# A mixture of softmaxes on one core: the first unit is loaded in one transfer of four heads instead of four transfers of one head

## The chip, the core and the metric

The kernel runs on one core of one Trainium2 chip. Its engines work side by side, each through its own list of instructions: TensorE for matmuls (PE in the profile, with PEld for its weight loads), VectorE (DVE), ScalarE (ACT), GpSimd (POOL) and SyncE (SP), which does no arithmetic and issues transfers. The transfers themselves are run by 16 DMA engines between HBM and the core's memory. The metric is the device time of one execution in microseconds (us); lower is better.

## What is computed

```python
batch, seq, vocab, num_heads = 32, 128, 4096, 4
# logits: (batch, seq, heads, vocab) f32, prior: (batch, seq, heads) f32
prior_probs = np.exp(prior - prior.max(axis=-1, keepdims=True))
prior_probs = prior_probs / prior_probs.sum(axis=-1, keepdims=True)
softmax = np.exp(logits - logits.max(axis=-1, keepdims=True))
softmax = softmax / softmax.sum(axis=-1, keepdims=True)
mixture = np.sum(prior_probs[..., None] * softmax, axis=2)   # over the 4 heads
```

For each of 32 x 128 rows, four rows of 4096 logits (the heads) become four softmaxes, which are added with the weights of a softmax over `prior`. The input is 32 x 8 MiB and the output 32 x 2 MiB. There is little arithmetic for each byte.

## The kernel before, in words

A *unit* u is one of the 32 batch entries: 128 rows on the 128 partitions, with four heads of 4096 f32 (16 KB a row and head, 2 MiB a head). `ring` is a buffer of 12 slots of one head each, so it holds three units. Head h of unit u lies in slot 4u + h modulo 12, except the very last head. `acc` is the whole PSUM, 128 x 4096 f32: one unit's sum. Columns are cut in four quarters of 1024, and a matmul covers 512 of them.

The order of all work is written by hand as a text of words. A word is a letter, digits, and a unit: `'` is the unit before, `+2` the unit two later, `@26` unit 26, and nothing is the unit of the text itself. The letters and their lines:

- **L** (`load`, line 120): loads heads a to b on SP's queue. Heads whose slots lie side by side go in one transfer; `L` alone is all four heads, `L03` heads 0 to 2, `L34` head 3 alone. **S** (`store`, line 125) stores the unit; for units 2 to 21 on ACT's queue, otherwise on SP's.
- **M** (`peak`, line 128, DVE): the negated maximum of one head. **E** (`exp`, line 133, ACT): the exponential of one head in place, with its sum. **R** (`recip`, line 139, DVE): the reciprocal of the sum.
- **G** (`diagonal`, line 142, POOL): a 128 x 128 diagonal matrix of the row weights prior / sum. **X** (`weigh`, line 151, PE): adds one head, times that matrix, into `acc`; heads 0 to 2 go this way.
- Head 3: **C** (line 158, POOL) makes its row weight and **Z** (line 162, POOL) scales its later columns.
- Joining: for the first quarter or two, **A** (line 168, DVE) adds head 3 and `acc`. For the other quarters **V** (line 187, ACT) copies `acc` out and **P** (line 190, POOL) adds the scaled head 3. Both write into the slot of head 3, and from there the unit is stored.

Each text handles heads of unit u and joins unit u - 1 in between. For unit 1 the text is:

```python
"M0 E0 R3' C3' Z314' M1 R0 G0 A01' V12' P12' V23' P23' V34' P34' E1 X0 S' L03+2 L34+2 "
"M2 E2 R1 G1 X1 M3 E3 R2 G2 X2 "
```

An engine takes the instructions of its own letters in this order. So on SP the store of unit u - 1 comes after its last P, then the loads of unit u + 2, which go into the slots that unit u - 1 leaves: `L03+2` behind the joins, `L34+2` behind the end of the store. From unit 24 on the order is a longer list of words with unit numbers.

Ahead of the texts, line 208 runs the words in `FIRST` for unit 0. Line 209 issues the load of `prior` on ACT's queue. Line 210 loads unit 1 with `L`. Lines 218 to 228 compute the prior's softmax, five steps on DVE and one on ACT, and transpose it to `pp` on DVE. All this stands ahead of `M0` of unit 0 in DVE's list. The text for unit 0 then has `L03+2 L34+2`, the loads of unit 2, which need no free slot and so wait for nothing.

Of the kernel before, what the change touches and what calls it, by code (L numbers as in the profile page):

```python
# [22 lines left out]

FIRST = "L01 L12 L23 L34"
STEADY = (
    "M0 E0 R3' C3' Z324' M1 R0 G0 A01' A12' V23' P23' V34' P34' E1 X0 S' L03+2 L34+2 "
    "M2 E2 R1 G1 X1 M3 E3 R2 G2 X2 "
# [43 lines left out]
def kernel(  # L73
# [124 lines left out]
    def run(u, words):  # L198
        for w in words.split():
            op, digits, back, on, at = re.fullmatch(  # L200
                r"([A-Z])(\d*)('*)(?:\+(\d+))?(?:@(\d+))?", w
            ).groups()
            v = int(at) if at else u - len(back) + int(on or 0)
            if 0 <= v < U:
                step[op](v, *map(int, digits))

    with tc.manual_schedule():
        run(0, FIRST)
        nc.scalar.dma_start(out=pr, in_=prior)
# [53 lines left out]
```

## Time and profile before

| | |
|---|---|
| median of 3 runs | 787.47 us (787.11 to 787.48) |
| the profiled execution | 786.99 us |
| its span, from the first instruction to the last | 785.2 us |
| busiest engines, share of the span | PE 86%, DVE 82%, ACT 70%, POOL 38% |
| moved by DMA | 335.90 MB, 428 GB/s over the span |
| granted TensorE clock, mean | 0.965 |

Times in the views count from the span's start. A row of the timeline has the start, the duration, the engine, the line, the operation, what it writes and reads, how often it is merged into that row, and in brackets how long the engine sat idle before it and what ended that. A row of DMA issues has what is moved, the queue, how often, the size of each, and the median time from issue to landing. In the list of queues, a row has the number of packets, the MB, and the share of 16 engines' time that the packets took.

### The profile page before, as it was taken

To read this page: it belongs to the slowest core of one execution; us is meant where nothing else is said; L and a number is where in the kernel's file an instruction comes from. 1 tells how busy PE (TensorE), PEld (TensorE's weight loads), DVE (VectorE), ACT (ScalarE), POOL (GpSimd) and SP (SyncE) were. 2 spreads that over 40 slices of the span, in tenths; PEclk is the share of its full clock that TensorE was granted. 3 is DMA by queue.
4 is the path that set the end of the run, shared out by engine and by line. 5 is a ranking of instruction groups with operands and counts; after the bars stand their busy time and mean duration, and the time that the engine had idled before them with its cause. 6 is when DMAs were issued, how large, how long until landed. Compare 5 with 4: busy or idle time off the path is not lost.

```text
span 785.2 us, 4590 instructions
## 1 busy us (share of the span) xinstructions
PE 679.0 (86%) x1508; PEld 291.8 (37%) x1508; DVE 644.2 (82%) x326; ACT 548.0 (70%) x327; POOL 296.9 (38%) x244
## 2 busy tenths in 40 slices
PE   0959998888998989989889898998978998899996
PEld 0424444333443333434334333343333433334342
DVE  6489877897778977779877798777888877979895
ACT  2566876867668666687676776766857668779883
POOL 0053333433134332334323343323430544277892
PEclk9979999999999999989999999999989999999999
DMA  9999999999999999999999999999999999999998
GB/s 377 451 417 426 452 416 423 431 446 430 437 417 432 440 437 437 427 420 437 444 422 446 410 435 451 425 431 420 432 440 442 425 418 431 444 419 429 429 427 340
DMA packets 15336, 335.90 MB, mean 428 GB/s; under 512 B 1713, under 2 KB 1713, under 8 KB 2257
## 3 DMA queue, kind: packets, MB, share of 16 engines
q1 hardware_dynamic: 12384, 293.61, 87.1%
q10 hardware_dynamic: 2928, 42.01, 12.5%
q8 instruction: 12, 0.20, 0.1%
q14 instruction: 12, 0.09, 0.0%
HBM read 268.50 MB, written 67.11 MB: 427 GB/s over the span
## 4 chain that ended last, share of the span: by engine, by line
DMA 58%; DVE 12%; PE 10%; POOL 10%; issue 6%; ACT 3%; SPq 0%; POOLq 0%; ACTq 0%
DMA ring<-in_logits_dram 58%; DVE nmax L128 12%; PE acc L151 10%; POOL ring L190 7%; ACT ring L187 2%; ACT ring L133 1%; POOL ring L184 1%; POOL ring L162 1%; POOL diag L142 1%; DVE ring L168 0%; SPq L120 0%; DVE rden L139 0%; SPq L125 0%; POOLq L190 0%; POOLq L142 0%
## 5 line engine op out<-in xcount | busy, mean ns | idle before, releaser
L151 PE MATMUL acc<-ring,diag 128*128 128x512 f32 x1508 | 679.0, 611 | 99.3 <-ACT ring L187 63.7
L128 DVE TENSOR_REDUCE nmax<-ring 128x1 f32<-128x4096 f32 x128 | 563.1, 4409 | 115.9 <-DMA ring<-in_logits_dram 115.9
L133 ACT ACTIVATE ring<-ring,nmax 128x4096 f32<-128x4096 f32 x128 | 474.6, 3708 | 203.7 <-DVE nmax L128 203.3
L151 PEld LDWEIGHTS acc<-ring,diag 128*128 128x128 f32 x1508 | 291.8, 196 | 485.6 <-issue 356.3
L190 POOL TENSOR_TENSOR ring<-ring 128x1024 f32<-128x1024 f32 x69 | 162.3, 2371 | 19.6 <-ACT ring L187 12.9
L142 POOL TENSOR_SCALAR diag<-ident,rden,pp 128x128 f32<-128x128 f32 x96 | 42.9, 448 | 237.5 <-DVE rden L139 237.5
L158 POOL TENSOR_TENSOR wght<-rden,pp 128x1 f32<-128x1 f32 x33 | 6.2, 189 | 209.5 <-DVE rden L139 209.5
L187 ACT ACTIVATE ring<-acc 128x1024 f32<-128x1024 f32 x69 | 67.4, 1010 | 16.2 <-PE acc L151 12.0
L162 POOL TENSOR_SCALAR ring<-ring,rden,pp 128x2048 f32<-128x2048 f32 (+3 forms) x35 | 75.1, 2146 | 9.4 <-DVE rden L139 9.4
L168 DVE SCALAR_TENSOR_TENSOR ring<-ring,wght,acc 128x1024 f32<-128x1024 f32 x59 | 73.2, 1270 | 3.0 <-PE acc L151 1.3
L139 DVE RECIPROCAL rden<-dsum 128x1 f32<-128x1 f32 x128 | 19.3, 153 | 10.1 <-ACT ring L133 10.1
L133 ACT ACTIVATION_READ_ACCUMULATOR ring<-ring,nmax 128x1 f32 x128 | 24.2, 189 | 0.0
L184 POOL TENSOR_TENSOR ring<-ring 128x1024 f32<-128x1024 f32 x5 | 11.9, 2373 | 0.1
L218 DVE TENSOR_REDUCE pmax<-pr 32x128 f32<-32x512 f32 x1 | 0.7, 674 | 5.2 <-DMA pr<-in_prior_dram 5.2
L220 ACT ACTIVATE pr<-pr 32x512 f32<-32x512 f32 x1 | 0.6, 628 | 4.1 <-DVE pr L219 4.1
L168 DVE SCALAR_TENSOR_TENSOR ring<-ring,wght 128x1024 f32<-128x1024 f32 x2 | 2.5, 1283 | 0.3 <-POOL wght L158 0.3
L220 ACT ACT_TABLE_LOAD x1 | 1.3, 1283 | 1.2 <-PEq L247 1.2
L227 DVE STREAM_TRANSPOSE pp<-pn 32x128 f32<-32x128 f32 x4 | 1.2, 302 | 0.1
L221 DVE TENSOR_REDUCE pmax<-pr 32x128 f32<-32x512 f32 x1 | 0.7, 674 | 0.7 <-ACT pr L220 0.7
L223 DVE TENSOR_TENSOR pn<-pr,pmax 32x512 f32<-32x512 f32 x1 | 1.0, 1021 | 0.0
L222 DVE RECIPROCAL pmax<-pmax 32x128 f32<-32x128 f32 x1 | 0.9, 942 | 0.0
L219 DVE TENSOR_TENSOR pr<-pr,pmax 32x512 f32<-32x512 f32 x1 | 0.7, 680 | 0.0
(6 smaller groups left out, 0.9 us busy)
## 6 DMA issues: line engine op xcount, KB each, us to landing
ring<-in_logits_dram SPq DMA_DIRECT2D x27, 6144.0 KB, 34.3
ring<-in_logits_dram SPq DMA_DIRECT2D x43, 2048.0 KB, 25.9
out_dram<-ring ACTq DMA_DIRECT2D x20, 2048.0 KB, 16.0
out_dram<-ring SPq DMA_DIRECT2D x11, 2048.0 KB, 14.0
out_dram<-ring SPq DMA_DIRECT2D x4, 512.0 KB, 5.5
pr<-in_prior_dram ACTq DMA_DIRECT2D x1, 64.0 KB, 4.4
ring<-in_logits_dram SPq DMA_DIRECT2D x1, 39.4
```

The lines of the kernel that those rows point to most:

```text
L128: nc.vector.tensor_reduce(out=nmax[:, u, h : h + 1], in_=slot(u, h), op=ALU.max, axis=AX.X, negate=True)
L133: nc.scalar.activation(slot(u, h), slot(u, h), AF.Exp, bias=nmax[:, u, h : h + 1], accum_out=dsum[:, u, h : h + 1],)
L139: nc.vector.reciprocal(rden[:, u, h : h + 1], dsum[:, u, h : h + 1])
L142: nc.gpsimd.tensor_scalar(out=diag[:, u % 2, h], in0=ident, scalar1=rden[:, u, h : h + 1], scalar2=pp[:, h, u : u + 1], op0=ALU.mult, op1= ...
L151: nc.tensor.matmul(acc[:, k * W : (k + 1) * W], lhsT=diag[:, u % 2, h], rhs=e[:, k * W : (k + 1) * W], start=h == 0, stop=h == H - 2 or (u ...
L158: nc.gpsimd.tensor_mul(wght[:, u, h : h + 1], rden[:, u, h : h + 1], pp[:, h, u : u + 1])
L162: nc.gpsimd.tensor_scalar(out=e, in0=e, scalar1=rden[:, u, h : h + 1], scalar2=pp[:, h, u : u + 1], op0=ALU.mult, op1=ALU.mult,)
L168: nc.vector.scalar_tensor_tensor(out=o, in0=slot(u, h, a, b), scalar=wght[:, u, h : h + 1], in1=more, op0=ALU.mult, op1=ALU.add,)
L184: nc.gpsimd.tensor_add(e, e, slot(u, 2, a, b))
L187: nc.scalar.activation(slot(u, 1, a, b), acc[:, a * C : b * C], AF.Copy)
L190: nc.gpsimd.tensor_add(home(u, a, b), slot(u, 1, a, b), slot(u, 3, a, b))
L220: nc.scalar.activation(pr, pr, AF.Exp)
```

## The change

`FIRST` held four words, one for each head of unit 0. It now holds one word for all four heads:

```diff
-FIRST = "L01 L12 L23 L34"
+FIRST = "L"
```

`load` (line 115) joins heads whose slots lie side by side, and unit 0's four heads are in slots 0 to 3:

```python
while h + n < to and place(u, h + n) == s + n:
    n += 1
nc.sync.dma_start(out=ring[:, s : s + n], in_=logits[u, :, h : h + n, :])
```

SP's list therefore begins with one transfer of 128 rows of 64 KB, the form that unit 1 has in both kernels, where it had four transfers of 128 rows of 16 KB. All heads of unit 0 now wait for the end of this one transfer. SP issues 3 instructions fewer. Instructions of the other engines, and their order, are the same in both kernels; only which transfer's semaphore they wait for differs.

## The prediction, as recorded before the result was known

> **What bounds the kernel now.** I read the page first, for what is full; then the chain of waits, for what is late each round; then the first 72 us of the timeline, the only place that the diff touches; then the DMA issues and packets there.
>
> ```profile
> DMA  9999999999999999999999999999999999999998
> PEclk9979999999999999989999999999989999999999
> HBM read 268.50 MB, written 67.11 MB: 427 GB/s over the span
> ```
>
> The DMA engines are at 90% or more in every slice but the last. The same list of queues asked for 20 to 760 us alone says more:
>
> ```profile
> DMA packets 13713, 319.22 MB, mean 431 GB/s; under 512 B 1520, under 2 KB 1520, under 8 KB 1520
> q1 hardware_dynamic: 10810, 276.99, 87.0%
> q10 hardware_dynamic: 2880, 41.94, 13.3%
> ```
>
> 87.0 + 13.3 is all of the 16 engines' time: there is no gap to speak of between 20 and 760 us. The chain of waits repeats one round of 48.5 us for two units, 34.3 us of it a load waiting in this queue. So the time is what the queue needs for its bytes, plus its start and its end. A change in the first microseconds counts only if it alters the time that rows take in the queue, or if it makes the queue run dry later. An engine that is late costs nothing as long as a transfer is queued.
>
> The start, from the timeline of 0 to 75 us:
>
> ```profile
> 5.23 0.67 DVE L218 TENSOR_REDUCE pmax<-pr 32x128 f32<-32x512 f32 x1 [5.23 <-DMA pr<-in_prior_dram]
> ...
> 11.33 8.75 DVE L128 TENSOR_REDUCE nmax<-ring 128x1 f32<-128x4096 f32 x2
> ...
> 20.84 22.34 PE L151 MATMUL acc<-ring,diag 128*128 128x512 f32 x48 [20.84 <-POOL diag L142]
> ...
> 24.45 4.40 DVE L128 TENSOR_REDUCE nmax<-ring 128x1 f32<-128x4096 f32 x1
> ...
> 42.33 4.42 DVE L128 TENSOR_REDUCE nmax<-ring 128x1 f32<-128x4096 f32 x1 [13.41 <-DMA ring<-in_logits_dram]
> ...
> 50.49 2.83 ACT L187 ACTIVATE ring<-acc 128x1024 f32<-128x1024 f32 x3
> ...
> 51.72 7.00 POOL L190 TENSOR_TENSOR ring<-ring 128x1024 f32<-128x1024 f32 x3
> ...
> 58.75 0.35 SPq L125 DMA_DIRECT2D out_dram<-ring  x1
> ...
> 59.26 8.11 SPq L120 DMA_DIRECT2D ring<-in_logits_dram  x2
> ```
>
> The reader is to see the slack. The prior's steps keep DVE to 11.33. Then the four maxima of unit 0 (the last at 24.45) run without a wait for data, and after 28.85 DVE is idle for 13.41 us until unit 1 lands. Joining unit 0 (lines 187 and 190) starts only behind unit 1's first maxima and exponential, at 50.49. Unit 0's store is issued at 58.75 and the first load of unit 3 at 59.26: the first moment at which the queue depends on any compute.
>
> **What the transfers cost.** Three rows of DMA issues, each from a short window around its issue (at 2.15, 3.65 and 4.05 us), and the queue in 10 to 20 us and in 24 to 40 us:
>
> ```profile
> ring<-in_logits_dram SPq DMA_DIRECT2D x1, 2048.0 KB, 20.8
> ```
>
> ```profile
> ring<-in_logits_dram SPq DMA_DIRECT2D x1, 6144.0 KB, 53.4
> ring<-in_logits_dram SPq DMA_DIRECT2D x1, 2048.0 KB, 57.8
> ```
>
> ```profile
> q1 hardware_dynamic: 299, 4.37, 102.7%
> ```
>
> ```profile
> q1 hardware_dynamic: 112, 7.34, 106.0%
> ```
>
> Head 3 of unit 0, issued at 2.15, lands at 22.95; unit 2 lands at 57.0 and 61.9. Of the 299 packets, 32 are the 4-byte ends of transfers, so a 16 KB row takes 1.027 x 160 / 267 = 0.615 us of one engine. A 64 KB row takes 1.060 x 256 / 112 = 2.42 us. A transfer has 128 rows, eight for each engine.
>
> **The change, part by part.**
>
> 1. *Bytes.* Unit 0 takes 4 x 8 x 0.615 = 19.69 us of each engine now and 8 x 2.42 = 19.38 us as one transfer: -0.3 us for the queue, and all behind it lands 0.3 us earlier. The single end marks are about 0.01 us each, nothing. Bounds: 0 (startup, where rows take longer than later, may eat it) and -0.4. I take -0.3, as unit 1 shows that very form. Unit 0 then lands at 22.65 and unit 1 at 42.0.
>
> 2. *SP's issues.* Three fewer, of 0.33 to 0.7 us each in SP's list; all seven are through by 4.40, and the queue has work until 61. Hidden; the cover is the queue itself. The first transfer starts its rows about 1.0 us after its issue at 0.79 (first packets at 1.8 in the trace), and that stays.
>
> 3. *The prior's load* is the one thing that shares the start. Its 32 rows of 2 KB, two on each engine, and an end mark each took a turn between 16 KB rows, and it lands 4.4 us after its issue. Turns between 64 KB rows cost up to three times 2.42 - 0.615 = 1.8 us more, 5.4 in all: it lands at 10.6, and DVE's 6.1 us (5.23 to 11.33) end at 16.7. A fourth turn makes it 19. Both are before 22.65. Hidden, with 4 to 6 us to spare.
>
> 4. *Unit 0's work* starts at 22.65 instead of 11.33: 11.3 us late. The maxima end at 40.2 instead of 28.85, still before unit 1 lands at 42.0, so DVE takes unit 1 on time. ACT ends unit 0's last exponential at about 43.9, before unit 1's first at 46.5. PE is what comes late: its 48 matmuls run from 32.1 to 54.5 instead of 20.84 to 43.18. The second quarter of columns is done eight matmul records (0.43 us each at full clock, from the spacing of the weight loads) before the end, at 51.1, where ACT could have copied it at 50.2. So the three copies start at 51.1, 52.8 and 54.5, not back to back, and ACT's next exponential moves by 2.3 us. POOL's first add starts at 52.05 instead of 51.4 (both with the 0.3 us of part 1); the other two follow without a wait, since each takes 2.34. Unit 0's store is issued at about 59.1 instead of 58.75.
>
> 5. *Is the queue still full then?* The last rows of unit 2 leave the first engine at 60.93 (the 16 end marks lie between 60.93 and 61.28 in the packets), now 60.6. A store issued at 59.1 has rows ready 1.0 us later, by the one row for that, the first transfer of the run: 60.1. Half a microsecond is left of what was 1.2. No gap, +0. Bounds: 0 and +0.5, if the issue takes half as long again and the estimate of 59.1 is 0.5 us early.
>
> 6. *What is late next.* Queued behind the late copies on ACT are unit 1's exponentials, and DVE waits for them: 2.3 us. PE gains it back. In the row of stretches below it sat idle from 43.2 to 52.6, and its granted clock is 0.50 from 48 to 57, about ten matmuls at 0.86 us. With unit 1 directly behind unit 0 at 54.5 there is no such pause; 48 x 0.43 = 20.6 brings it to 75.1, where it ends at 75.26 now. Unit 1's store, at 80.40 now, hangs on that, and the queue then has work until head 3 of unit 3 lands at 88.7. DVE's 2.3 us go into its idle time at 70 to 80 (2.7 us). Nothing reaches the queue: +0.
>
> ```profile
> 48.00:50.00 2.00, 0.00 (x0) 0.00 (x0) 2.00 (x1) 2.00 (x1) 1.97 (x1) 0.50 0.91 393
> ```
>
> The end of the program is the same work at the same distance from the last bytes, so it moves with the queue. Sum: 785.2 - 0.3 = 784.9 of span, with the 1.8 us around it 786.7; the profiled execution was 0.5 below the median of the three runs, so **787.2** as a median.
>
> **The rivals.**
>
> *The prior is starved, and the kernel is slower.* If the prior's rows do not get their turn until an engine is through its eight rows of unit 0, the prior lands at about 22.5 and DVE starts unit 0 at 28.6, 17.3 us late instead of 11.3. The copies and adds move by 6.0, the store to 65.1, its rows to 66.1: the queue is dry for 5.5 us, and the time is 792.7. It decides as soon as the prior lands after 16.5. Against it: between 16 KB rows, with 32 of them queued on each engine ahead, the prior landed after 4.4 us. [...] The Trainium skill (DMA: Bandwidth & Descriptors, section Queues, rings and completion order) says that an engine drains a whole packet, typically 9 to 17 descriptors, from one queue before it goes to the next. With eight rows on each engine that would be this rival; the packets of this trace are single rows, and turns came after each. Chance 0.08.
>
> *The queue runs dry at unit 0's store* for a smaller reason: unit 0 lands later than 22.65 or its chain is slower. Half a microsecond is covered, and every further one costs one. To be seen as slower (over 0.2%, 1.6 us, about what a measurement of this kernel can tell from no change) it takes a store at 61.2. Time 789.2, chance 0.08. Most smaller cases are within 0.2%.
>
> *Fewer transfers are worth more, and the kernel is faster.* The first transfer landed 7.5 us after issue, of which 4.9 are rows; if each hand-over between transfers cost those 2.6 us, three fewer give 779.7. The heads of unit 0 land at 8.3, 13.1, 18.2 and 22.95 (issue plus time to landing), hardly more apart than the 4.9 us of their rows, so a hand-over costs about nothing. Chance 0.05.
>
> **How the numbers follow.** My forecast, hidden with -0.3 us, has 0.79; its own range, from the bounds of parts 1 and 5, and the spread of the three runs, is 786.4 to 788.1. To hold 8 in 10 the range reaches into the dry queue: 786.2 to 789.2. Faster by over 0.2% has 0.06 (the hand-over, and what I have not seen), slower 0.15 (the two slow rivals, less the small end of one), the same 0.79.
>
> **What the profile of the changed kernel would show.** The first maximum (line 128) starts at about 22.6 with a DMA wait before it; the second wait for unit 1, now 13.41 us, shrinks to about 2. The prior's first step starts between 10 and 13: after 16.5 the first rival holds. PE's clock has no dip between 47 and 57. Unit 0's store is issued at about 59.1 and unit 3's first load lands near 82.4 (82.7 now); if it lands past 83.5, the queue ran dry. I am wrong if unit 0 lands after 24.5, if the prior comes late, or if the later rounds are not fixed by the queue alone.

## The result, and the profile after

The change makes the kernel a little slower: 788.29 us median (787.36 to 789.38, 20 runs) against 787.11 us (786.50 to 787.89, 20 runs), a ratio of 1.0016 with a 95% interval of 1.0010 to 1.0022. That is 1.2 us. It lies within the 0.2% that I had set as no change and within the range, but clear of noise, and on the other side of the 0.3 us gain that I had forecast.

The profiled execution after took 787.88 us, its span 786.2 us, 1.0 us more than before. DMA engines and clock look as before on the page; the difference has to be looked for in the first 70 us. The landings first, from the page and from a short window around the first issue:

```profile
pr<-in_prior_dram ACTq DMA_DIRECT2D x1, 64.0 KB, 10.5
```

```profile
ring<-in_logits_dram SPq DMA_DIRECT2D x1, 22.6
```

Unit 0, issued at 0.79, lands at 23.4 (22.95 for its last head before, 22.65 forecast). The prior lands at 11.3 and is not in the way. Then the timeline of the start:

```profile
23.39 8.74 DVE L128 TENSOR_REDUCE nmax<-ring 128x1 f32<-128x4096 f32 x2 [6.03 <-DMA ring<-in_logits_dram]
...
32.91 49.32 PE L151 MATMUL acc<-ring,diag 128*128 128x512 f32 x110 [32.91 <-POOL diag L142]
...
42.75 4.42 DVE L128 TENSOR_REDUCE nmax<-ring 128x1 f32<-128x4096 f32 x1 [1.77 <-DMA ring<-in_logits_dram]
...
52.28 1.02 ACT L187 ACTIVATE ring<-acc 128x1024 f32<-128x1024 f32 x1 [1.28 <-PE acc L151]
...
53.45 7.01 POOL L190 TENSOR_TENSOR ring<-ring 128x1024 f32<-128x1024 f32 x3 [1.28 <-ACT ring L187]
...
60.50 0.35 SPq L125 DMA_DIRECT2D out_dram<-ring  x1
```

It goes as forecast as far as unit 1, which DVE takes on time after a wait of 1.77 us. PE no longer pauses between the units. But the first copy of unit 0 waits for PE until 52.28, the adds run from 53.45, and the store is issued at 60.50: 1.75 us later than before, where I had said 0.35. What this does to the queue is in the stretches 61.0 to 62.5 and 65 to 67 us, before and then after; the last two columns are the DMA engines' share and the GB/s:

```profile
61.00:62.50 1.50, 1.50 (x5) 0.70 (x4) 1.50 (x3) 0.94 (x1) 0.45 (x1) 1.00 1.15 492
65.00:67.00 2.00, 2.00 (x6) 0.81 (x5) 2.00 (x3) 1.42 (x3) 0.94 (x2) 1.00 1.26 524
```

```profile
61.00:62.50 1.50, 1.50 (x5) 0.74 (x4) 1.50 (x1) 1.50 (x1) 0.12 (x1) 1.00 0.88 371
65.00:67.00 2.00, 2.00 (x6) 0.85 (x5) 2.00 (x1) 2.00 (x1) 0.45 (x1) 1.00 1.27 385
```

At 61, where the queue passes from the loads of unit 2 to the store of unit 0, it moves 371 GB/s instead of 492, and at 65 to 67, the end of that store, 385 instead of 524. The single packets in the trace say what it is: the engines that are through first sit idle for up to 0.3 us at 61, and the last two rows of the store take 0.8 and 1.1 us on average (1.2 at most) instead of 0.61. From the last 4-byte end mark of unit 2 to that of the store it takes 5.82 us instead of 4.95. The queue was not to be without work before unit 0's store, and this is where it was.

### The profile page after: what moved, and what is told of

It reads as the page before. It is cut to its first block, busy times and chain, and to the rows that moved or that the text cites. A ratio compares the mean times of both kernels' runs of the same rounds, so it can differ in the third digit from the quotient of the medians.

```text
span 786.2 us, 4582 instructions
## 1 busy us (share of the span) xinstructions
PE 677.5 (86%) x1508; PEld 291.3 (37%) x1508; DVE 643.9 (82%) x326; ACT 548.3 (70%) x327; POOL 296.9 (38%) x244
## 4 chain that ended last, share of the span: by engine, by line
DMA 60%; DVE 13%; POOL 10%; PE 7%; ACT 5%; issue 5%; SPq 0%; POOLq 0%
DMA ring<-in_logits_dram 60%; DVE nmax L128 12%; POOL ring L190 7%; PE acc L151 7%; ACT ring L133 3%; ACT ring L187 2%; POOL ring L184 1%; POOL ring L162 1%; POOL diag L142 1%; DVE ring L168 0%; DVE rden L139 0%; SPq L125 0%; POOLq L190 0%; POOLq L142 0%
## 5 line engine op out<-in xcount | busy, mean ns | idle before, releaser
L218 DVE TENSOR_REDUCE pmax<-pr 32x128 f32<-32x512 f32 x1 | 0.7, 674 | 11.3 <-DMA pr<-in_prior_dram 11.3
```

## Experiments

**Which part of the change is it?** Two theories stood against each other. *Late start*: with all heads of unit 0 behind one landing, its store comes when the queue is about to run dry. *Row form*: rows of 64 KB at the start, or the prior between them, cost time themselves (unit 0's last end mark was at 22.93 in this trace, 22.49 before). I ran both kernels again, and two that part these.

The kernel before, unchanged:

> The kernel before, unchanged, beside itself: ratio 1.000, within 0.0005 either way. Its trace tells which stretched rows of the DMA queue come back from run to run: unit 0's store and head 3 of unit 3 (64 to 67 us and 84 to 88 us) were stretched by 0.1 and 0.25 us in the first trace of before, and by 0.8 and 1.1 us in the trace of the change. If they were chance, they move in this trace; if they hang on when the store is issued, they stay small here.

Measured: 1.0000 (0.9991 to 1.0009). Store issued at 58.77, unit 0's last end mark at 22.51, the same two places hardly stretched. It is the same kernel twice, and in this second trace the stretches are where they were and as small.

The change, unchanged:

> The change, unchanged, for a second trace: ratio 1.001 to 1.002 again. Late-start theory (the store of unit 0 comes to the queue just as it runs out): store issued at about 60.5, unit 0's store and head 3 of unit 3 stretched again by 0.8 and 1 us. Chance theory: the stretches are elsewhere or gone, and only the 0.4 us of unit 0's landing is left.

Measured: 1.0019 (1.0010 to 1.0028). Here the store is issued at 61.24, and the hole is plain:

```profile
61.24 0.35 SPq L125 DMA_DIRECT2D out_dram<-ring  x1
```

```profile
61.00:62.50 1.50, 1.50 (x5) 0.69 (x4) 1.34 (x2) 1.50 (x3) 0.66 (x2) 1.00 0.42 175
65.00:67.00 2.00, 2.00 (x6) 0.82 (x5) 2.00 (x3) 1.33 (x1) 0.45 (x1) 1.00 1.28 393
```

175 GB/s: the last end mark of unit 2 is at 61.24 and the store's first row starts at 62.09, 0.85 us after its issue. And unit 0's last end mark is at 22.46 in this trace: the later landing of the first trace does not come back, while the slowness does.

Four loads of one head, with head 0 last:

```diff
-FIRST = "L01 L12 L23 L34"
+FIRST = "L34 L23 L12 L01"
```

> Four loads of one head for unit 0 as before, but head 0 last: work on unit 0 starts at 22.95 as in the change, while the rows stay 16 KB and the prior lands at 5.2. Late-start theory: the store is issued at 60.1 to 60.5 and the kernel is slower by 0.5 to 0.8 us (ratio 1.0006 to 1.0010), the change's loss less the 0.4 us of the landing. Row theory (64 KB rows at the start cost the time): ratio 1.000, within 0.0004.

Measured: 1.0017 (1.0008 to 1.0026), the whole of the change's loss and more than I had left for it, with 16 KB rows and the prior on time. Work starts at 23.00, the store is issued at 60.87, the queue moves 350 GB/s in 61.0 to 62.5 and 262 in 65 to 67. The row theory falls.

Two loads of two heads:

```diff
-FIRST = "L01 L12 L23 L34"
+FIRST = "L02 L24"
```

> Unit 0 in two loads of two heads (32 KB rows): work starts at about 13.2, the third maximum at about 22.7 instead of 20.06, so unit 0's store stays at 58.7 to 59.0. Late-start theory: no more than the landing's share, ratio 1.000 to 1.0003. Row theory: about half of the change's loss, ratio 1.0006 to 1.0009, with unit 0 landing 0.2 us later than in the kernel before.

Measured: 0.9999 (0.9990 to 1.0008). Work starts at 13.25, the third maximum waits 0.88 us for its load, and the store is issued at 58.73. Half the transfers, and over the eleven executions nothing lost. The one that was profiled was the slowest of them, 787.85 us. In its trace the last two rows of the store of unit 0 took 0.7 and 0.8 us on average, and head 3 of unit 3 ended about 1 us later than in the kernel before. So rows can stretch without a late store; a late store makes it the rule.

**Does a late start cost as such, or only through the store?** Five more runs. Head 0 third, so that work starts at 18.2:

```diff
-FIRST = "L01 L12 L23 L34"
+FIRST = "L23 L12 L01 L34"
```

> Head 0 of unit 0 is loaded third: its work starts at 18.2, 6.9 us later than before and 4.8 us earlier than in the change. Dry-queue theory: PE is through unit 0 at 50 to 51.5 us, no copy waits for it, the store stays at 58.7 to 58.8, and the ratio is 1.000 within 0.0005: nothing of 6.9 us is paid. Rival, every late microsecond costs its share: 6.9 of 11.6 of the change's loss, ratio 1.0010.

Measured: 0.9999 (0.9990 to 1.0008), store at 58.96. PE's end moves by 6.9 us and nobody waits for it: of a loss in proportion there is no sign.

The kernel before with its start on time, but two copies and adds of unit 0 behind an exponential of unit 1 (in the text for unit 1):

```diff
-... A01' V12' P12' V23' P23' V34' P34' E1 X0 S' L03+2 L34+2 "
+... A01' V12' P12' E1 V23' P23' V34' P34' X0 S' L03+2 L34+2 "
```

> The kernel before, with unit 0 loaded by heads and started at 11.3, but two of unit 0's copies and adds moved behind unit 1's second exponential, so that its store is issued at 60.7 to 61.3. Dry-queue theory: the queue has a gap of 0.5 to 1 us after 61, the store's last rows are stretched, and the ratio is 1.0010 to 1.0018, as if the start had been late. Rival (the late start itself costs): 1.000 within 0.0005.

Measured: 1.0031 (1.0019 to 1.0043, six executions), more than expected; the direction is as the dry queue has it. Why it costs more than the change, with a store as late, no run here tells. The store is issued at 61.02:

```profile
61.02 0.35 SPq L125 DMA_DIRECT2D out_dram<-ring  x1
```

```profile
61.00:62.50 1.50, 1.50 (x5) 0.55 (x4) 1.50 (x3) 1.24 (x1) 0.85 (x2) 1.00 0.52 218
65.00:67.00 2.00, 2.00 (x6) 0.95 (x5) 2.00 (x3) 1.41 (x2) 1.24 (x2) 1.00 1.15 336
```

The same hole and the same stretched end, without any change to the loads of unit 0.

The change with its late start, but unit 0 joined on DVE in all four quarters:

```diff
-    "M0 E0 R3' C3' Z314' M1 R0 G0 A01' V12' P12' V23' P23' V34' P34' E1 X0 S' L03+2 L34+2 "
+    "M0 E0 R3' C3' M1 R0 G0 A01' A12' A23' A34' E1 X0 S' L03+2 L34+2 "
```

> The change, with unit 0 joined in all four quarters on DVE and none through ACT and POOL: the start stays late (23), but the store can go at 57.0 to 58.0, before the queue runs out at 61. Dry-queue theory: no gap, ratio 1.000 within 0.0005. Rival (late start costs in another place too): 1.0012 to 1.0019, as the change.

Measured: 1.0000 (0.9991 to 1.0009). Work starts at 22.88, as late as in the change, and the loss is gone. The join no longer goes through POOL, whose three adds took 7.0 us in a row:

```profile
51.03 3.64 DVE L168 SCALAR_TENSOR_TENSOR ring<-ring,wght,acc 128x1024 f32<-128x1024 f32 x3
...
54.93 1.28 DVE L168 SCALAR_TENSOR_TENSOR ring<-ring,wght,acc 128x1024 f32<-128x1024 f32 x1 [0.26 <-PE acc L151]
...
56.30 0.35 SPq L125 DMA_DIRECT2D out_dram<-ring  x1
```

The store goes at 56.30, earlier than expected and 5.0 us ahead of unit 2's first end mark, at 61.33. A second run of it:

> The change with unit 0 joined on DVE, again: store issued at 56 to 58, no gap, ratio 1.000 within 0.0005. If the late start costs beside the store, it is 1.001 or more in one of the two.

Measured: 0.9995 (0.9986 to 1.0004), store at 56.65.

The kernel before with that join:

> The kernel before with the same join on DVE: store at about 56.3 instead of 58.75. Dry-queue theory: the queue was full anyway, ratio 1.000 within 0.0005, and the comparison with the run above is then level. Rival (an earlier store is a gain of its own): up to 2.4 us faster, ratio 0.997.

Measured: 1.0004 (0.9995 to 1.0013), store at 56.15. An earlier store is no gain where the queue was full.

**Where does it begin to cost?** Only the last copy and add behind the exponential:

```diff
-... V34' P34' E1 X0 S' L03+2 L34+2 "
+... E1 V34' P34' X0 S' L03+2 L34+2 "
```

> As the late-store run, with only the last copy and add of unit 0 behind unit 1's second exponential: store issued at 59.4 to 59.8, 0.7 to 1.0 us later than before, and its rows ready 0.85 us after that, at 60.3 to 60.6, just before the first engine is through unit 2 (60.9). Dry-queue theory: no gap, the store's last rows not longer than before, ratio 1.000 within 0.0005. Rival (every late microsecond of this store costs): about 40% of the late-store run, ratio 1.0012.

Measured: 1.0014 (1.0005 to 1.0023), where I had expected nothing. Store at 59.57, and no hole: 470 GB/s in 61.0 to 62.5. Again:

> The milder late store again, for a second trace and time, since the first was slower (1.0014) with no gap in the queue. Gap theory: the 1.0014 was chance, now 1.000 to 1.0005. Lateness theory (a store that comes within 1.5 us of the queue's end stretches its last rows even without a gap): ratio 1.0006 to 1.0016 again, no gap after 61, and the store's last end mark at 66.6 to 67.0 instead of 66.2 to 66.4.

Measured: 1.0010 (1.0001 to 1.0019), store at 59.56:

```profile
61.00:62.50 1.50, 1.50 (x5) 0.74 (x4) 1.50 (x3) 1.29 (x1) 0.45 (x1) 1.00 0.97 415
65.00:67.00 2.00, 2.00 (x7) 0.80 (x6) 2.00 (x3) 1.41 (x2) 1.28 (x2) 1.00 1.48 500
```

The store's last end mark is at 66.74, as the lateness theory had it.

So the loss begins before the queue is empty. Sorted by when the store is issued, with the time from unit 2's end marks to the store's (the middle one of 16 engines, from the packets of each trace; the ratio is that of all executions, not of the one traced):

| kernel | store issued, us | store's time in the queue, us | ratio to before |
|---|---|---|---|
| joined on DVE, before | 56.15 | 4.86 | 1.0004 |
| joined on DVE, change (two runs) | 56.30, 56.65 | 4.86, 4.86 | 1.0000, 0.9995 |
| two loads of two heads | 58.73 | 5.09 | 0.9999 |
| before (two traces) | 58.75, 58.77 | 4.92, 4.95 | 1.0000 |
| head 0 third | 58.96 | 4.91 | 0.9999 |
| last add late (two runs) | 59.57, 59.56 | 5.10, 5.31 | 1.0014, 1.0010 |
| the change (two traces) | 60.50, 61.24 | 5.74, 6.68 | 1.0016, 1.0019 |
| head 0 last | 60.87 | 6.34 | 1.0017 |
| two adds late | 61.02 | 6.36 | 1.0031 |

Of the 1.8 us that the second trace of the change loses here (6.68 against 4.92), about 1.1 is the hole at 61 and the rest the stretched rows at the store's end. Head 3 of unit 3, the load ahead of the next store, is stretched too: with the delay of the store included, its middle end mark is 2.1 to 2.7 us later than before in the four traces with a store after 60, and 1.0 to 1.2 us in the two at 59.6. It is about 1 us later with two loads of two heads too, so this second stretch does not hang on unit 0's store alone. What is lost by 142 us then stays: the last engine's end mark is behind that of the first trace of before by 1.04 us at the end of the load that leaves the queue at 141.9 there, and by 1.14 at the end of the run; in its second trace by 2.05 and 2.06.

## Why the prediction was wrong, point by point

*The bound* was right. The queue is full from 1.8 us on, and what the start costs is what it loses there. That DVE takes unit 1 on time, that the prior is hidden, and that PE makes up its delay by 80 us (unit 1's store at 80.50, 80.40 before) all came as forecast.

*Part 1, the bytes: -0.3 us, not seen.* The price of a 64 KB row, 2.42 us, came from unit 1, in a queue that was running. The first three of unit 0 took 3.10, 2.62 and 2.58 us on average, while before it was the first 16 KB row alone that took long, 1.18 us. That is 1.0 us of start instead of 0.6 and eats the gain; the first bound of this part, 0, was the right one. The last end mark of unit 0 is at 22.42 to 22.93 in the four traces with one transfer (22.46 in the second of the change) and at 22.49 to 22.61 in the eight with four.

*Part 4, the store at 59.1: this is the step that failed.* It was issued at 60.50 and 61.24. Three terms were short, together by 1.4 and 2.1 us. Unit 0 landed 0.7 and 0.3 us later than 22.65. PE was slow for longer at its start: weight loads 0.85 us apart, where 0.43 is full speed. (The column of the granted clock reads 1.00 there; the spacing is what shows it.) Before, then the two traces of the change:

```profile
22.71 0.34 PEld L151 LDWEIGHTS acc<-ring,diag 128*128 128x128 f32 x1 [0.52 <-issue]
23.56 0.33 PEld L151 LDWEIGHTS acc<-ring,diag 128*128 128x128 f32 x1 [0.52 <-issue]
24.14 0.19 PEld L151 LDWEIGHTS acc<-ring,diag 128*128 128x128 f32 x1 [0.24 <-issue]
```

```profile
35.63 0.34 PEld L151 LDWEIGHTS acc<-ring,diag 128*128 128x128 f32 x1 [0.52 <-issue]
36.49 0.28 PEld L151 LDWEIGHTS acc<-ring,diag 128*128 128x128 f32 x1 [0.52 <-issue]
37.00 0.19 PEld L151 LDWEIGHTS acc<-ring,diag 128*128 128x128 f32 x1 [0.24 <-issue]
```

```profile
37.74 0.34 PEld L151 LDWEIGHTS acc<-ring,diag 128*128 128x128 f32 x1 [0.52 <-issue]
38.59 0.21 PEld L151 LDWEIGHTS acc<-ring,diag 128*128 128x128 f32 x1 [0.52 <-issue]
39.05 0.19 PEld L151 LDWEIGHTS acc<-ring,diag 128*128 128x128 f32 x1 [0.24 <-issue]
```

PE began at 32.91 and 32.46 and reached full speed at 37.00 and 39.05, after 4.1 and 6.6 us; in the trace that I took the 22.34 us from it was 3.3 us (20.84 to 24.14). That is the shortest of all thirteen traces; the same kernel's second trace has 5.9 us. The first trace held a warning too: its next start, at 52.61, reached full speed only at 58.37, after 5.8 us. The first copy came 28.9 and 30.1 us after the first maximum began, where I had 28.45. I treated as fixed a time that differs by more than a microsecond from run to run; in the kernel before nobody waited for it, so it had never mattered. The Trainium skill (TensorE: Matmul & The Clock Gate, Part 1) has PE start at half its clock until a window of about 3.4 us has been busy, and the window runs free, so that the switch comes at a different point in each run. That agrees in kind; the 3.3 to 6.6 us of these traces are a wider spread than the half microsecond that it gives. Last, POOL's first add began 1.17 us after the copy, where I had put 0.95; the row of before has 1.23 (50.49 to 51.72), so this was a slip in the sum.

*Part 5, "half a microsecond is left": wrong in its sum and in its price.* With the right store time nothing is left: rows are ready 0.85 us after the issue (I had 1.0), at 61.35 and 62.1, and the engines were through unit 2 at 61.0 to 61.7 and 60.7 to 61.2. But I had also priced a store that comes just in time at nothing, and a gap at its own length. The runs at 59.6 show about 0.9 us lost with no gap at all, and those with a gap have stretched rows beside it. So the rule I began with, that a late engine costs nothing as long as a transfer is queued, did not hold at this place. No row of the trace of before showed a store that close to the queue's end. An estimate from these rows: even with the short start of PE, a landing at 22.95 puts the store at 59.6 (22.95 + 28.45 + 1.17 + 7.0), where those runs still lost. The sign that I had named for a dry queue, unit 3's first load landing past 83.5, was too coarse: it landed at 83.2 and 84.3.

*The rivals.* The one to which I gave 0.08, a queue that runs dry at unit 0's store, is what happened, at its named place and with a size under the 2.0 us that I gave it; the mistake was in its chance. The starved prior did not come: it landed at 11.3 and 10.8, three turns of 64 KB rows as worked out, and the first maximum waited 6.03 us for unit 0 after the prior's steps were done. Hand-overs between transfers cost nothing that shows: two loads instead of four gave 0.9999, and in the packets of unit 0's four loads each engine's next row starts within 0.01 us of the end mark ahead of it.

*What stays open.* Why the last rows of that store, and then rows of head 3 of unit 3, take up to twice their time when the store comes late, and why they did so once, with two loads of two heads, when it did not. In the runs with the join on DVE it was the last rows of unit 2, ahead of the store, that stretched, by 0.4 to 0.6 us on average, and the store itself ran clean (4.86 us), at no loss to be measured. Both are ends of transfers at which the queue turns between loads and stores; which property of the issue decides where it falls, no run here tells. That the late store costs through its place in the queue is shown from both sides: made late alone it costs (1.0010 to 1.0031), made early under the late start it does not (1.0000, 0.9995).

## What to carry to other kernels

When a queue is the bound, delay elsewhere is free only up to the moment at which the queue next needs something from compute: find that issue, work out its slack against the queue's end, and add up every duration on the way with the spread that it has between runs, not the value of one trace. A slack that an engine never used, as PE's slow start here, is no constant. And leave more than the bare time: here a store issued 1.3 to 1.5 us before the first engine was through already cost 0.9 us, while 2.0 to 2.2 us before was free.

## What was not expected of the hardware

- A transfer issued to a queue without other work has its first row 0.84 to 0.85 us after its issue (four traces; 1.0 us for the first transfer of a run), and the first rows of a run take longer than later ones: by 0.4 to 0.6 us with rows of 16 KB, by 0.7 with rows of 64 KB.
- PE's weight loads stayed 0.85 us apart, twice the 0.43 of full speed, for 3.3 to 6.6 us after its first matmul, in thirteen traces of identical or nearly identical kernels.
- Rows of 16 KB, which take 0.61 us, took up to twice that towards the end of the store of unit 0, or of a load just ahead of a store, and averaged up to 1.1 us over the 16 engines. This cost up to about 1 us at one place. It was there in every trace with a late store. In the three with the join on DVE it lay ahead of the store, and once, with two loads of two heads, it was as large without a late store.
